# A decoder layer on one core: attention's long scans in two parts, two weight blocks prepared earlier, and other banks for the first down product

## The chip, the cores and the metric

The kernel runs on one core of a Trainium2 chip. Its engines each have their own instruction queue: TensorE (PE, with PEld for its weight loads), VectorE (DVE), ScalarE (ACT), GpSimd (POOL) and SyncE (SP, which here issues nearly all DMAs). The metric is the device time of one execution in microseconds.

## The reference

One layer on 1024 tokens of width 1024, all in float32: an SSD (Mamba-2) head group and a stick-breaking attention head group in parallel, their outputs joined and projected, then an MLP, then a last norm. What the change touches:

```python
logits = jnp.einsum("bthd,bshd->bhts", qb, kb) * scale      # a block of 128 queries, all keys up to them
log_beta = jax.nn.log_sigmoid(logits)
log_1m_beta = jnp.where(mask, jax.nn.log_sigmoid(-logits), 0.0)
suffix = lax.cumsum(log_1m_beta, axis=-1, reverse=True) - log_1m_beta
att = jnp.where(mask, jnp.exp(log_beta + suffix), 0.0)      # then att @ v
...
x = x + jnp.concatenate([y_ssd, y_att], axis=-1) @ w_out
h = rmsnorm(x, norm_mlp_g)
x = x + jnp.square(jax.nn.relu(h @ w_up)) @ w_down
return rmsnorm(x, final_norm_g)
```

## The kernel before

**Products.** Every large product is made of three matmuls on float32r halves (high x high, high x low, low x high). An operand is split by a copy to float32r (the high half) and a subtraction (the low half): `split(raw, hi, lo, where)`, L105, with the copy on ACT and the subtraction on DVE ("vec") or POOL ("poollo"), or both on POOL ("pool").

**Order.** The program is written for a scheduling framework that puts each engine's instructions into one fixed queue ahead of time, by program order, by priorities (`tc.high_priority` pulls an instruction forward) and by when it reckons them ready; waits between engines are semaphores. On the chip each queue runs in order. So an instruction that is cut into two can also change the places of its neighbours in the queue.

**Stages.** Projection, convolution and SSD come first. Then attention, in eight pairs of heads (`hp`): for each pair the queries are worked on in groups `g` of two 128-query blocks, while PE interleaves the projection of the next pair's q, k and v (`qkv`, matmuls L161 to L163). In attention, the logits go to PSUM (L528 to L531), ACT makes `m` = sigmoid(-logit) (L548) and `a` = sigmoid(logit) (L549), DVE runs a reversed running product over `m` in place (the scan, L539), and multiplies `a` by it (L541). PE then transposes `a` (L599) into a bank of the tag `tr` (two banks), ACT copies out the high half `ath` (L602), DVE makes the low half `atl` (L603), and PE multiplies with v (L615, L616) into a bank `ps_b` (two banks), which DVE's `yt` (L629) empties. L602, L603 and L629 are of high priority. For `g` = 1 a tile holds two heads of 384 or of 512 columns; for `g` = 2 and 3 a tile holds one head of 640, 768, 896 or 1024 columns, and the logits of its columns from 512 on go through PSUM and ACT first. `short` has scans of 128 and 256 columns. So a pair has two scans each of the eight lengths.

**Mix.** The joined output is projected in eight blocks (`mix_block`, L734 to L736); L783 adds each result to the residual `x1`. In the last block (7) the first half of the rows is normed as it is finished (`norm_a`, `norm_b`) and transposed into `B11` and `B21` (`block`, L858 to L862).

**MLP.** Up and down products are Strassen-like products P1 to P7 of 512-wide blocks. The up product runs over `steps`; the first 12 (`pre`) are the P1 and P2 of the first six blocks, while the remaining operands (T1 to T4, B22) are still being made by `block_sums`, `norm_b` and `block` in `second_half`. `wblock` makes the weight operand of a step: a load of a whole row block `wf` (1024 columns, two buffers), and a split of 512 of them. The results are squared by ACT (L950, L951) and, with sums by DVE (`u_sums`, L970), written to memory (`ub`). The pools `prb` (before) and `pe` (after) share memory, as do the PSUM banks of the tags `tr`, `x`, `y` and the six banks `a` of the down product. `mm` has two banks of its own for the whole kernel; in the up product P1 and P2 use them.

**Down product.** Seven products P1, P2, P5, P6, P7, P3, P4, each with four banks and 16 operands `n` (two blocks each: `raw` from `ub`, and a block of w_down). Operands 0 to 3 are made before the up product ends. `prepare(n)` issues loads nine ahead and makes operands six ahead. `load_t(kp)` loads a block that product P5 needs; for operands 4 to 15 of P1 it is also P1's own.

Of the kernel before, what the change touches and what calls it, by code (L numbers as in the profile page):

```python
# [8 lines left out]
F32 = mybir.dt.float32  # L9
F32R = mybir.dt.float32r  # L10
BF16 = mybir.dt.bfloat16
AF = mybir.ActivationFunctionType
ALU = mybir.AluOpType
# [3 lines left out]
P = 128  # L17
# [7 lines left out]
NW = 4  # L25
# [25 lines left out]
def trunk(ctx: ExitStack, tc, x, wct, wdt, cols, g_mix, g_mlp, g_fin, wout, wup, wdown, out):  # L51
    nc = tc.nc
    mm, act, vec, pool = nc.tensor.matmul, nc.scalar, nc.vector, nc.gpsimd
# [14 lines left out]
    ws = ctx.enter_context(tc.tile_pool(name="ws", bufs=2))  # L68

    def bank(tag):  # L70
        if tag == "mm":
            return psm.tile([P, 512], F32, name="ps_mm", tag="mm")
        n, w = banks[tag]
        return banks["pool"].tile([P, 512 * w], F32, name=f"ps_{tag}", tag=tag, bufs=n)
# [30 lines left out]
    def split(raw, hi, lo, where):  # L105
        if where == "pool":
            pool.tensor_scalar(out=hi, in0=raw, scalar1=1.0, scalar2=0.0, op0=ALU.mult, op1=ALU.add)  # L107
            pool.tensor_tensor(out=lo, in0=raw, in1=hi.bitcast(F32), op=ALU.subtract)  # L108
        else:
            act.copy(out=hi, in_=raw)  # L110
            e = vec if where == "vec" else pool
            e.tensor_tensor(out=lo, in0=raw, in1=hi.bitcast(F32), op=ALU.subtract)  # L112
# [13 lines left out]
    def rms_scale(ss, r):  # L126

        pool.tensor_scalar(out=r, in0=ss, scalar1=1.0 / 1024.0, scalar2=EPS, op0=ALU.mult, op1=ALU.add)
        pool.tensor_tensor(out=r, in0=r, in1=mhalf[:, : r.shape[-1]], op=ALU.pow)
# [383 lines left out]
    class Group:  # L513
# [19 lines left out]
        def weigh(self, a, m, segments):  # L533

            end = sum(segments)
            cut = end
            for k in segments[::-1]:
                mv = m[:, cut - k:cut][:, ::-1]
                vec.tensor_tensor_scan(mv, mv, mv, 1.0, ALU.mult, ALU.min)  # L539
                cut -= k  # L540
            vec.tensor_tensor(out=a[:, 0:end - 1], in0=a[:, 0:end - 1], in1=m[:, 1:end], op=ALU.mult)  # L541

# [140 lines left out]
    for k in range(len(slots) + LATE):  # L683
        if k < len(slots):
            n, r, b = slots[k]
# [92 lines left out]
    def mix_block(b, operands, lag=0):  # L778


        def store(ps, tt, n):
            o, c = x1[tt][:, n], (0 if b < 4 else 8) + tt
            vec.scalar_tensor_tensor(out=o, in0=ps, scalar=rr[:, c:c + 1], in1=o, op0=ALU.mult, op1=ALU.add)  # L783

        return accumulate(*operands, store, lag)
# [43 lines left out]
    def norm_a(tt):  # L829

        sq = pr.tile([P, D], F32, name="sq", tag="sq")
        ss = pr.tile([P, 1], F32, name="ss", tag="ss", bufs=4)
        r = pr.tile([P, 1], F32, name="r", tag="r", bufs=4)
        nc.sync.dma_start(out=x1d[tt], in_=x1[tt])
        act.activation(out=sq, in_=x1[tt], func=AF.Square, accum_out=ss)
        rms_scale(ss, r)
        scale[tt] = r

    def norm_b(tt):

        vec.scalar_tensor_tensor(out=x1[tt], in0=x1[tt], scalar=scale[tt][:, 0:1], in1=gm, op0=ALU.mult, op1=ALU.mult)
# [13 lines left out]
    def block(nm, src, j, tag):  # L855
        ps = bank(tag)
        for k in range(4):
            nc.tensor.transpose(out=ps[:, k * P:(k + 1) * P], in_=src[:, k * P:(k + 1) * P], identity=ident)  # L858
        pv = ps.rearrange("p (k t) -> p k t", k=4)
        dh, dl = [h[:, :, j * P:(j + 1) * P] for h in hb[nm]]  # L860
        act.copy(out=dh, in_=pv)
        vec.tensor_tensor(out=dl, in0=pv, in1=dh.bitcast(F32), op=ALU.subtract)  # L862

    scale = {}
    pc_.close()
    pr = pr_.enter_context(tc.tile_pool(name="pr", bufs=1, side="right", reuse_waits="tile"))
    gm = pr.tile([P, D], F32, name="gm", tag="gm")
# [2 lines left out]
    for i, _ in enumerate(mix_block(7, nxt)):  # L870
        for tt in range(4):
            if i == 2 * tt + 3:
                norm_a(tt)
            if i == 2 * tt + 4:
                norm_b(tt)
            if i == 2 * tt + 6:
                block("B11", x1[tt][:, k0], tt, "tr")
                block("B21", x1[tt][:, k1], tt, "tr")
        if i in (11, 13):
            norm_a(i // 2 - 1)  # L880
    norm_b(4)
    block("B11", x1[3][:, k0], 3, "tr")
    block("B21", x1[3][:, k1], 3, "tr")
# [7 lines left out]
    def second_half():  # L891

        turn = ("tr", "x", "y") * 7
        for tt in range(4, 8):
            made = block_sums(tt)
            if tt < 7:
                norm_b(tt + 1)
            for n, (nm, src) in enumerate(made):
                block(nm, src, tt - 4, turn[5 * (tt - 4) + n])
                if (5 * (tt - 4) + n) % 2:  # L900
                    yield
# [6 lines left out]
    for m in range(0, 16, 2):  # L908
# [1 line left out]
        if m < EARLY:  # L910
            head = [(m, "P6"), (m + 1, "P6")]
        steps += head + [(m + e, p) for p in ("P7", "P5", "P4", "P3") for e in range(2)]
    wraw, wsum, wop, acc, kept = {}, {}, {}, {}, {}
    loaded = set()

    def wload(i, name, early):
# [111 lines left out]
    def b_of(kp, nm):  # L1028
        return wdown[2 * kp + int(nm[1]) - 1][:, (int(nm[2]) - 1) * 512:int(nm[2]) * 512]
# [6 lines left out]
    def load_t(kp):  # L1036
        t_of[kp] = pe.tile([P, 512], F32, name="t", tag="t", bufs=16)
        nc.sync.dma_start(out=t_of[kp], in_=b_of(kp, "B11"))

    def d_load(n, pl, bufs):  # L1040

        p, kp = slots[n]
        a = load_raw(ub[UB[A_OF[p]] + kp], pl, bufs)
        b = None
        if p == "P1":
            if n < 4:
                b = load_raw(b_of(kp, "B11"), pl, bufs)
            else:
                load_t(kp)
        elif p == "P6":  # L1050
            b22_of[kp] = pe.tile([P, 512], F32, name="b22", tag="b22", bufs=16)
            nc.sync.dma_start(out=b22_of[kp], in_=b_of(kp, "B22"))
        elif p != "P3":
            b = load_raw(b_of(kp, {"P2": "B21", "P5": "B12", "P7": "B12", "P4": "B21"}[p]), pl, bufs)
        braw[n] = a, b
# [26 lines left out]
        split(b, o[2], o[3], "vec")  # L1082
        bops[n] = o

    loaded_ops = set()
    blocks = second_half()
    pu, pu_ = None, ExitStack()
    for s in range(len(pre)):
# [29 lines left out]
    gf = pr.tile([P, D], F32, name="gf", tag="gm")  # L1118
    psum_phase(a=(6, 1))

    def final_norm(tt):
        sq = pr.tile([P, D], F32, name="sq", tag="sq")
        ss = pd.tile([P, 1], F32, name="ss", tag="ss", bufs=4)
        r = pd.tile([P, 1], F32, name="r", tag="r", bufs=4)
        act.activation(out=sq, in_=x2[tt], func=AF.Square, accum_out=ss)
        rms_scale(ss, r)
        vec.scalar_tensor_tensor(out=x2[tt], in0=x2[tt], scalar=r[:, 0:1], in1=gf, op0=ALU.mult, op1=ALU.mult)
        nc.sync.dma_start(out=out[tt * P:(tt + 1) * P, :], in_=x2[tt])
# [32 lines left out]
    later2 = []  # L1161
    NRAW, LOAD, MAKE, TAIL = 8, 9, 6, 4
    loads = made = len(bops)
    for kp in range(4):
        load_t(kp)
    nc.sync.dma_start(out=gf, in_=g_fin)

    def prepare(n):
        nonlocal loads, made
        while loads < min(n + LOAD + 1, len(slots)):  # L1170
            d_load(loads, pe, NRAW)
            loads += 1
        while made < min(n + MAKE + 1, len(slots)):
            d_make(made)
            made += 1

    def d_mm(ps, tt, o, first, last):
        t = slice(tt * P, (tt + 1) * P)
        mm(out=ps, lhsT=o[0][:, t], rhs=o[2], start=first, stop=False)  # L1179
        mm(out=ps, lhsT=o[0][:, t], rhs=o[3], start=False, stop=False)  # L1180
        mm(out=ps, lhsT=o[1][:, t], rhs=o[2], start=False, stop=last)  # L1181

    for j, p in enumerate(ORDER):
        pss = [bank("mm" if j % 2 and tt > 1 else "a") for tt in range(4)]
        end = 16 - (TAIL if p == "P4" else 0)
        for kp in range(end):
            n = 16 * j + kp
            prepare(n)
            if kp > 0 and later2:
                later2.pop(0)()  # L1190
            o = bops.pop(n)
            for tt in range(4):
                d_mm(pss[tt], tt, o, kp == 0, kp == 15)
        for tt in range(4):
            for kp in range(end, 16):
                d_mm(pss[tt], tt, bops[16 * j + kp], False, kp == 15)
            done(p, tt, pss[tt])
            if p == "P4" and tt > 0:
                final_norm(3 + tt)
            if p == "P4" and tt == 3:  # L1200
                sq = pr.tile([P, D], F32, name="sq", tag="sq")
                for n, ac in ((n2, last_sums[1]), (n1, last_sums[0])):
                    act.activation(out=sq[:, n], in_=x2[7][:, n], func=AF.Square, accum_out=ac)
# [71 lines left out]
```

## Time and profile before

| | us |
|---|---|
| three runs, median (lowest to highest) | 1777.83 (1775.32 to 1777.92) |
| the profiled execution, its own time | 1772.97 |
| its span, first to last instruction | 1771.3 |
| PE busy in the span | 1710.7 |
| DVE busy | 1276.8 |
| ACT busy | 813.8 |
| POOL busy | 518.5 |

The mean granted TensorE clock is 0.993 of full speed. PE is busy for 97% of the span, so some 60 us are left in which it does nothing; nearly 27 us of them lie in the first 40 us and the last 20 us (PE busy 26.66 of 40.00 and 9.46 of 20.00), which the change doesn't touch. A time is read best against PE's waits, stage by stage.

### The profile page before, as it was taken

Reading aid. Unit: us, or ns where it says so; the run is one execution under the profiler, and the core shown is the slowest. Engines: PE = TensorE matmul, PEld = TensorE weight load, DVE = VectorE, ACT = ScalarE, POOL = GpSimd, SP = SyncE. Lnnn points to the kernel's source line nnn. Section 1 sums busy time; section 2 is a strip of 40 time slices with the busy share of each in tenths; the row PEclk is TensorE's granted clock in tenths of the full one; section 3 lists DMA queues with packets and bytes.
Section 4 is the critical chain, followed back from the end, with each engine's and each line's share of the span. In section 5 each row is a group of like instructions: output and inputs, shape, how many; then the busy total and the mean of one; then the engine's idle time right before and its main releaser. Section 6 shows DMA issues by size and latency. Waiting matters only on the chain.

```text
span 1771.3 us, 23843 instructions
## 1 busy us (share of the span) xinstructions
PE 1710.7 (97%) x8492; PEld 1396.8 (79%) x8492; DVE 1276.8 (72%) x1771; ACT 813.8 (46%) x1560; POOL 518.5 (29%) x601
## 2 busy tenths in 40 slices
PE   6999999998999999999999999999999999999997
PEld 5778878877778778778778888788888877888886
DVE  6587887459888888888775666967665656687775
ACT  5233133336667666666563121554455446444443
POOL 6222222053443443443464332410222200010221
PEclk9999999999999999999999999999999999999999
DMA  4101102130101100110135221455434449855454
GB/s 157 37 27 57 54 31 96 36 119 25 34 31 34 33 31 33 34 36 28 60 122 210 103 89 71 159 167 208 156 143 143 159 155 320 281 167 153 162 167 148
DMA packets 90839, 189.39 MB, mean 107 GB/s; under 512 B 10080, under 2 KB 14432, under 8 KB 90720
## 3 DMA queue, kind: packets, MB, share of 16 engines
q1 hardware_dynamic: 90576, 187.61, 31.1%
q8 instruction: 67, 1.10, 0.3%
q14 instruction: 52, 0.43, 0.1%
q10 hardware_dynamic: 144, 0.26, 0.0%
HBM read 137.50 MB, written 50.33 MB: 106 GB/s over the span
## 4 chain that ended last, share of the span: by engine, by line
PE 81%; DVE 10%; POOL 2%; ACT 2%; DMA 2%; issue 2%; SPq 0%; DVEq 0%; POOLq 0%; ACTq 0%
PE ps_mm L161 8%; PE ps_mm L163 8%; PE ps_mm L162 8%; PE ps_a L1179 4%; PE ps_a L1181 4%; PE ps_a L1180 4%; DVE m L539 4%; PE ps_a L734 3%; PE ps_a L736 3%; PE ps_a L735 3%; PE ps_tr L599 3%; PE ps_x L987 3%; PE ps_x L985 3%; PE ps_x L986 3%; DVE a L541 2%; PE ps_mm L987 2%
## 5 line engine op out<-in xcount | busy, mean ns | idle before, releaser
L161 PE MATMUL ps_mm<-hhi,whi 128*128 128x512 f32 (+1 forms) x784 | 321.4, 410 | 0.0
L163 PE MATMUL ps_mm<-hhi,wlo 128*128 128x512 f32 (+1 forms) x784 | 308.4, 393 | 0.0
L162 PE MATMUL ps_mm<-hlo,whi 128*128 128x512 f32 (+1 forms) x784 | 307.5, 392 | 0.0
L539 DVE TENSOR_TENSOR_SCAN m<-m 128x512 f32<-128x512 f32 (+7 forms) x128 | 182.5, 1450 | 29.0 <-ACT m L548 28.4
L163 PEld LDWEIGHTS ps_mm<-hhi,wlo 128*128 128x128 f32 x784 | 148.2, 189 | 32.1 <-issue 2.4
L161 PEld LDWEIGHTS ps_mm<-hhi,whi 128*128 128x128 f32 x784 | 148.8, 190 | 19.8 <-issue 2.9
L162 PEld LDWEIGHTS ps_mm<-hlo,whi 128*128 128x128 f32 x784 | 149.0, 190 | 18.3 <-issue 1.5
L108 POOL TENSOR_TENSOR wlo<-raw,whi 128x512 fp32r<-128x512 f32 x90 | 138.3, 1537 | 7.4
L112 POOL TENSOR_TENSOR wlo<-wf,whi 128x512 fp32r<-128x512 f32 x48 | 65.4, 1364 | 243.2 <-ACT whi L110 243.2
L783 DVE SCALAR_TENSOR_TENSOR x<-ps_a,rr,x 128x512 f32<-128x512 f32 x128 | 93.7, 748 | 56.0 <-PE ps_a L736 46.8
L107 POOL TENSOR_SCALAR whi<-raw 128x512 fp32r<-128x512 f32 x90 | 67.9, 755 | 223.9 <-PE ps_mm L162 211.5
L603 DVE TENSOR_TENSOR atl<-ps_tr,ath 128x512 fp32r<-128x512 f32 (+1 forms) x160 | 100.6, 631 | 41.3 <-ACT ath L602 39.9
L110 ACT CAST op<-raw 128x512 fp32r<-128x512 f32 x131 | 78.0, 620 | 107.8 <-issue 48.4
L112 DVE TENSOR_TENSOR op<-raw,op 128x512 fp32r<-128x512 f32 x131 | 91.0, 716 | 37.3 <-ACT op L110 36.9
L1179 PE MATMUL ps_a<-op 128*128 128x512 f32 x278 | 109.0, 392 | 1.9 <-ACT uP L951 1.9
L1180 PE MATMUL ps_a<-op 128*128 128x512 f32 x278 | 108.8, 391 | 0.0
L1181 PE MATMUL ps_a<-op 128*128 128x512 f32 x278 | 108.7, 391 | 0.0
L548 ACT ACTIVATE m<-ps_a 128x384 f32<-128x384 f32 (+1 forms) x192 | 95.7, 498 | 25.0 <-PE ps_a L531 21.8
L599 PE MATMUL ps_tr<-ident,a 128*128 128x128 f32 x576 | 91.7, 275 | 14.3 <-DVE a L541 8.2
L602 ACT CAST ath<-ps_tr 128x512 fp32r<-128x512 f32 (+1 forms) x160 | 86.9, 545 | 35.9 <-PE ps_tr L599 34.0
L599 PEld LDWEIGHTS ps_tr<-ident,a 128*128 128x128 f32 x576 | 70.7, 140 | 37.5 <-DVE atl L603 9.5
L1136 POOL TENSOR_TENSOR x<-x,raw 128x512 f32<-128x512 f32 x16 | 26.4, 1657 | 248.5 <-DVE x L1144 113.9
(365 smaller groups left out, 4280.3 us busy)
## 6 DMA issues: line engine op xcount, KB each, us to landing
raw<-ub SPq DMA_DIRECT2D x112, 256.0 KB, 3.3
raw<-in_wct_dram SPq DMA_DIRECT2D x96, 256.0 KB, 2.6
wf<-in_wup_dram SPq DMA_DIRECT2D x38, 512.0 KB, 3.5
raw<-in_wdown_dram SPq DMA_DIRECT2D x68, 256.0 KB, 3.3
ub<-v SPq DMA_DIRECT2D x48, 256.0 KB, 2.0
raw<-in_wout_dram SPq DMA_DIRECT2D x32, 256.0 KB, 2.7
yl<-ygt SPq DMA_DIRECT2D x16, 512.0 KB, 4.4
ub<-uP SPq DMA_DIRECT2D x32, 256.0 KB, 2.0
```

The costliest lines, as they stand in the source:

```text
L108: pool.tensor_tensor(out=lo, in0=raw, in1=hi.bitcast(F32), op=ALU.subtract)
L112: e.tensor_tensor(out=lo, in0=raw, in1=hi.bitcast(F32), op=ALU.subtract)
L161: mm(out=o, lhsT=whi[:, wc], rhs=hhi[:, k, n], start=(k == 0), stop=False)
L162: mm(out=o, lhsT=whi[:, wc], rhs=hlo[:, k, n], start=False, stop=False)
L163: mm(out=o, lhsT=wlo[:, wc], rhs=hhi[:, k, n], start=False, stop=(k == KT - 1))
L539: vec.tensor_tensor_scan(mv, mv, mv, 1.0, ALU.mult, ALU.min)
L548: act.activation(out=m[:, o:o + w], in_=src, func=AF.Sigmoid, scale=-1.0)
L599: nc.tensor.transpose(out=tp[:, o:o + P], in_=a[:, c:c + P], identity=ident)
L603: vec.tensor_tensor(out=tl[:, o:], in0=tp[:, o:], in1=th[:, o:].bitcast(F32), op=ALU.subtract)
L1179: mm(out=ps, lhsT=o[0][:, t], rhs=o[2], start=first, stop=False)
L1180: mm(out=ps, lhsT=o[0][:, t], rhs=o[3], start=False, stop=False)
L1181: mm(out=ps, lhsT=o[1][:, t], rhs=o[2], start=False, stop=last)
```

## The change

Three edits. (1) In `weigh`, a scan of more than 384 columns becomes two: one over the last `h` columns from 1.0, then one over the others, which starts from the first one's last column, `m[:, cut - h]`. The lengths become 512 = 256 + 256, 640 = 256 + 384, 768 = 384 + 384, 896 = 384 + 512 and 1024 = 512 + 512 (the part that runs first is named first). (2) In the last mix block, after its turns 6 and 8, the weight operands of up steps 0 and 1 (P1 of blocks 0 and 1) are loaded into `raw` buffers and split, instead of at the start of the up product, from `wf`. The loads of `wf` stay for P2. (3) The first down product, and every second one after it, takes two `mm` banks and two `a` banks, and those between take four `a` banks; the loads `load_t(0)` to `load_t(3)` and of `gf` are moved from ahead of the product into its first turns, behind `prepare`.

```diff
@@ weigh
             for k in segments[::-1]:
-                mv = m[:, cut - k:cut][:, ::-1]
-                vec.tensor_tensor_scan(mv, mv, mv, 1.0, ALU.mult, ALU.min)
+                h = k // 256 * 128 if k > 384 else k
+                for p, start in ((cut - h, 1.0), (cut - k, m[:, cut - h:cut - h + 1]))[:1 + (h < k)]:
+                    mv = m[:, p:cut if p == cut - h else cut - h][:, ::-1]
+                    vec.tensor_tensor_scan(mv, mv, mv, start, ALU.mult, ALU.min)
                 cut -= k
@@ the last mix block
-    scale = {}
+    scale, wop = {}, {}
...
         if i in (11, 13):
             norm_a(i // 2 - 1)
+        if i in (6, 8):
+            raw = ws.tile([P, 512], F32, name="raw", tag="raw", bufs=2)
+            nc.sync.dma_start(out=raw, in_=wup[i - 6][:, 0:512])
+            hi = ws.tile([P, 512], F32R, name="whi", tag="whi", bufs=NW)
+            lo = ws.tile([P, 512], F32R, name="wlo", tag="wlo", bufs=NW)
+            split(raw, hi, lo, "poollo")
+            wop[i // 2 - 3] = hi, lo
...
-    wraw, wsum, wop, acc, kept = {}, {}, {}, {}, {}
+    wraw, wsum, acc, kept = {}, {}, {}, {}
...
-    loaded_ops = set()
+    loaded_ops = set(wop)
@@ the down product
-    for kp in range(4):
-        load_t(kp)
-    nc.sync.dma_start(out=gf, in_=g_fin)
...
     for j, p in enumerate(ORDER):
-        pss = [bank("mm" if j % 2 and tt > 1 else "a") for tt in range(4)]
+        pss = [bank("mm" if j % 2 == 0 and tt < 2 else "a") for tt in range(4)]
         end = 16 - (TAIL if p == "P4" else 0)
         for kp in range(end):
             n = 16 * j + kp
             prepare(n)
+            if n < 4:
+                load_t(n)
+            if n == 4:
+                nc.sync.dma_start(out=gf, in_=g_fin)
```

## Rows read from the trace of the kernel before

**Rows 1.** PE's waits, whole span: releaser, us in total, times, longest us

```profile
PE ps_tr L599 <- DVE a L541: 8.2, 10, 1.0
PE ps_tr L599 <- DVE atl L603: 6.1, 8, 1.7
PE ps_b L615 <- DVE yt L629: 5.9, 3, 2.8
...
PE ps_a L1179 <- ACT uP L951: 1.9, 1, 1.9
PE ps_x L858 <- DVE x L849: 1.7, 1, 1.7
...
PE ps_mm L987 <- POOL wlo L112: 1.6, 1, 1.6
PE ps_a L1179 <- ACT whi L110: 1.6, 1, 1.6
```

**Rows 2.** Windows, attention: stretch; us; PE, PEld, DVE, ACT, POOL busy; clock; DMA; GB/s

```profile
525.00:590.00 65.00, 62.95 (x368) 51.63 (x367) 54.82 (x67) 41.77 (x94) 27.17 (x39) 1.00 0.11 33
```

**Rows 3.** DVE's groups by shape: count, busy us, mean ns, idle before

```profile
L783 DVE SCALAR_TENSOR_TENSOR x<-ps_a,rr,x 128x512 f32<-128x512 f32 x128 | 93.7, 748 | 56.0 <-PE ps_a L736 46.8 <-POOL rr L129 8.5
...
L603 DVE TENSOR_TENSOR atl<-ps_tr,ath 128x512 fp32r<-128x512 f32 x96 | 65.5, 684 | 35.6 <-ACT ath L602 35.1
...
L539 DVE TENSOR_TENSOR_SCAN m<-m 128x1024 f32<-128x1024 f32 x16 | 37.6, 2351 | 0.0
...
L539 DVE TENSOR_TENSOR_SCAN m<-m 128x512 f32<-128x512 f32 x16 | 18.7, 1208 | 0.4 <-ACT m L548 0.4
...
L539 DVE TENSOR_TENSOR_SCAN m<-m 128x256 f32<-128x256 f32 x16 | 10.7, 668 | 0.0
```

**Rows 4.** Timeline of DVE in that pair: start us, us, instruction

```profile
571.27 2.81 DVE L539 TENSOR_TENSOR_SCAN m<-m 128x896 f32<-128x896 f32 x1 [0.92 <-ACT m L548]
574.19 1.09 DVE L541 TENSOR_TENSOR a<-a,m 128x895 f32<-128x895 f32 x1
...
575.79 2.28 DVE L539 TENSOR_TENSOR_SCAN m<-m 128x1024 f32<-128x1024 f32 x1
...
579.76 1.20 DVE L541 TENSOR_TENSOR a<-a,m 128x1023 f32<-128x1023 f32 x1
```

**Rows 5.** Timeline of POOL in the same stretch

```profile
570.92 1.28 POOL L108 TENSOR_TENSOR wlo<-raw,whi 128x512 fp32r<-128x512 f32 x1
...
575.84 3.33 POOL L108 TENSOR_TENSOR wlo<-raw,whi 128x512 fp32r<-128x512 f32 x1
```

**Rows 6.** Timeline of PE at the start of the up product

```profile
1126.58 0.66 PE L858 MATMUL ps_x<-ident,x 128*128 128x128 f32 x4 [1.73 <-DVE x L849]
...
1129.49 0.79 PE L987 MATMUL ps_mm<-B11h,wlo 128*128 128x512 f32 x1 [1.59 <-POOL wlo L112]
...
1132.64 0.42 PE L985 MATMUL ps_mm<-B11h,whi 128*128 128x512 f32 x1
```

**Rows 7.** Timeline of DVE there

```profile
1124.63 0.69 DVE L862 TENSOR_TENSOR B11l<-ps_tr,B11h 128x512 fp32r<-128x512 f32 x1 [0.30 <-ACT B11h L861]
```

**Rows 8.** Busy time of the engines (columns as in rows 2) in two stretches of 2 us

```profile
1130.00:1132.00 2.00, 2.00 (x6) 1.53 (x5) 2.00 (x4) 0.94 (x2) 1.50 (x2) 0.50 0.00 0
1454.00:1456.00 2.00, 2.00 (x6) 1.58 (x5) 1.54 (x3) 0.00 (x0) 0.00 (x0) 0.50 0.99 364
```

**Rows 9.** SP's queue at the start of the down product

```profile
1458.66 1.84 SPq L1038 DMA_DIRECT2D t<-in_wdown_dram  x4
...
1461.02 0.43 SPq L1038 DMA_DIRECT2D t<-in_wdown_dram  x1
```

**Rows 10.** PE there

```profile
1467.17 1.20 PE L1179 MATMUL ps_a<-whi 128*128 128x512 f32 x4 [1.58 <-ACT whi L110]
```

**Rows 11.** DMA issues of the whole kernel: count, KB each, median us to landing

```profile
raw<-ub SPq DMA_DIRECT2D x112, 256.0 KB, 3.3
```

**Rows 12.** The same between 1440 and 1480 us

```profile
t<-in_wdown_dram SPq DMA_DIRECT2D x16, 256.0 KB, 5.4
```

## The prediction

> **What bounds the kernel now.** I read the page first: PE is busy for 1710.7 of 1771.3 us, so no other engine sets the end, and a change is worth only what it takes from PE's idle time, or from the stretches in which PE's clock is low. Then PE's waits [rows 1], because each names the engine that came late; then the stretches around the three edits, for which of these waits lie there.
>
> In attention the waits are on DVE: for `a` (8.2 us in ten waits), for `atl` (6.1 in eight) and for `yt` (5.9 in three). The reader is to see in the window of one head pair [rows 2] how little that is: PE does nothing for 2.05 of 65 us. DVE is busy for 54.82, and from one long scan to the next product it has hardly a gap [rows 4]. So DVE isn't the bound there, but it is close to it, and what lengthens its queue in such a stretch reaches PE soon.
>
> At the start of the up product PE waits 1.7 us for DVE and 1.6 for POOL's `wlo`, at the start of the down product 1.9 for ACT's `uP` and 1.6 for ACT's `whi` [rows 1]. After the first two and after the 1.9 the granted clock falls to half (0.50, six matmuls in 2 us) [rows 8], so these stops cost more than the waits. After the second 1.6 I saw no such fall.
>
> **Edit 2, the first up operands: 3.5 us less.** In the queue of before, PE transposes T1 behind the wait for DVE, starts step 0 and stops again at its third matmul for `wlo` [rows 6]. With the operand there, the stop of 1.6 is gone. Step 0 also needs `B11l`, which ends at 1124.63 + 0.69 = 1125.32 [rows 7], while PE has been free since 1126.58 - 1.73 = 1124.85 [rows 6]. If the queue lets step 0 go ahead of T1, 0.5 of the 1.7 is left, a gain of 1.2. The half clock lasts from 1129.49 to 1132.64 [rows 6], 3.15 us, of which half, 1.6, is lost. Together 1.2 + 1.6 + 1.6 = 4.4. Against it: DVE is busy without a gap there (2.00 of 2.00) [rows 8], so PE, earlier by these microseconds, finds the next transposed blocks less ready; I take 0.9 off. What is added is two loads of 256 KB on SP (behind stores of `x1d` in program order, seven to nine turns of the mix block before its end), two casts on ACT, and two subtractions on POOL of the form that takes 1.28 [rows 5]. ACT and POOL have room in that stage. If POOL's two hold up DVE there, the last rows' norm comes up to 2.6 later, and that would eat most of the gain. Bounds: 0.5 to 4.4.
>
> **Edit 3, the first down product: 3.5 us less.** PE's first stop is for a bank whose last reader is ACT's square of the last up block (the 1.9). Before, one turn of three matmuls runs first. With two banks from `mm` and the one that was free before, three turns do, six matmuls more. The eight matmuls of the dip [rows 6] start 3.15 / 7 = 0.45 apart, so 0.225 at the full clock: six are 1.3. So 1.3 of the 1.9 goes, and the dip of the clock with it, which I cost like the other at 1.6: 2.9. Then the load of operand 4. Its `t` is issued at 1461.02, behind `gf` and four other `t` [rows 9], and PE gets it at 1467.17 [rows 10], 6.15 later. Without those ahead it could be issued where they were, at 1458.66, a gain of 2.36: PE gets it at 1464.8. With 1.5 MB less in flight (`gf` has 512 KB) the landing, 5.4 here [rows 12], should also come nearer to the 3.3 which such a load takes over the whole kernel [rows 11], by at most 2.1: 1462.7. PE, 2.9 earlier, asks for it at 1467.17 - 1.58 - 2.9 = 1462.7 too. So the end of this stop moves by 2.4 to 4.5, and it alone counts, since both stops lie in a row: I take 3.5. The moved loads are not wanted before P5 and the last norm; they cost nothing while loads run ahead of PE. Bounds: 0.5 (the loads wait for the memory of `prb` just as long, and the longer stop brings a dip) to 5.
>
> **Edit 1, the scans: 2 us less, and little certainty.** A pair has two scans each of 512, 640, 768, 896 and 1024 columns, so 80 are cut in all. Durations of the parts come from their own length [rows 3]: 2 x 668 - 1208 = 128 ns more for 512, 2 x 1208 - 2351 = 65 ns more for 1024. The second part must wait for the first: a product that depends on its scan starts 574.19 - (571.27 + 2.81) = 0.11 us after it [rows 4]. No row has a scan that starts from a column. The nearest is an operation with a column operand, 748 against 684 ns [rows 3], though it isn't the same operation; so 0 to 0.06. That makes 0.17 to 0.3 per cut, and I take 0.25: 20 us more of DVE's time in all, 2.5 in a pair, whose 54.82 then become some 57 of 65. I exclude a gain from faster scanning, as the parts' sum is above the whole.
>
> The errata section of the Trainium skill's page "VectorE: DVE Perf Modes" speaks against the cut: a fixed cost per instruction, about 150 cycles, is paid by each part. At 0.96 GHz that is an estimated 0.156 us, more than the 65 to 128 ns of the rows; 80 times it is 12.5 us, and the sum below would be about 1 us worse.
>
> What the cut gives is places in DVE's queue: `atl` and `yt` are of high priority and can now go between the parts instead of behind 2.28 us of scan [rows 4]. If that removes half of their 12.0 us of waits [rows 1], the gain is 6. What it costs is the product at the end: `a`, for which PE waits, ends at 579.76 + 1.20, and two cut scans are ahead of it in one gapless queue [rows 4]. That is 2 x 0.25 = 0.5 a pair, 4 in all. The early start of the part of 896 whose columns ACT makes first saves nothing, as POOL holds that scan up until 1.28 of its own are over [rows 4, 5]. Net 2 less; ends: 17 less (nearly all waits of DVE's three gone) to 12 more (the slow rival).
>
> **Sum.** 3.5 + 3.5 + 2 = 9 from the profiled execution's 1772.97 gives 1764. That execution is 4.9 below the median of the runs, 1777.83, so for the median 1769 (likeliest 1764 to 1774).
>
> **The rivals.** *DVE pays all back:* the cuts lengthen the gapless stretch, in which there are four (two of 512 follow), and all of it reaches PE: 8 x 4 x 0.25 = 8 us. Then -7 + 8 = +1: 1779, no change. For it is DVE's load [rows 2]; against it that PE idles only 2 us a pair today. Chance 0.19.
>
> *POOL comes in between (slower):* POOL's subtraction that began at 575.84 took 3.33 instead of 1.28 [rows 5], ending about 1.1 after the scan of 1024 [rows 4]: it stood still while the scan ran. And the scan of 896, begun while POOL was at work, took 2.81 [rows 4], more than 2.28 for 1024. The two exclude each other, instruction by instruction. A cut scan lets POOL in halfway, and the second part waits out 1.28. With the one scan of 1024 and the one of 896 ahead of `a` hit, that is 2 x 1.28 + 0.5 = 3.1 a pair at worst; less about 0.7 that DVE can fill with `atl`, 2.4: 8 x 2.4 = 19, so -7 + 19 = +12: 1790. It decides from 1.4 us a pair on (11 in all). Against it: the part for which POOL waits is the same work, and it only goes earlier, which shortens other stops. Chance 0.14. The Trainium skill's "SBUF — State Buffer", section "Who interferes with whom", states it as a rule: a VectorE instruction with two SBUF inputs and a GpSimd one that reads SBUF hold a shared port by turns, each for a whole instruction. The trace agrees with 3.33 against 1.28.
>
> *The gaps do all:* `atl`, `yt` and `a` come in time everywhere, 17 less beside 7: 1754. For it: the two of high priority no longer stand behind a whole scan; against it, `a` is not of high priority and its queue grows. Chance 0.12.
>
> *The early edits do nothing* (step 0 still goes behind T1 and the clock dips; the down loads wait for memory): 1 less instead of 7, with the scans' 2: 1775, within what can be told. Chance 0.05.
>
> **How the numbers follow.** The forecast has the rest, 0.50. A measurement of this kernel can tell some 0.2%, 3.6 us, from no change. Faster: 0.50 + 0.12 = 0.62, and 0.02 for the better half of the others' spread, 0.64; same 0.22; slower 0.14. The range leaves out most of the slow rival and half of the best: 1756 to 1784. It is this wide because of the scans alone.
>
> **What would show it.** In the changed profile: 80 more scans, pieces of 256 at 0.67, 384 near 0.9 and 512 at 1.2 us, with `atl` or `yt` between pieces. PE's waits on `atl` and `yt` down from 12 to about 6, on `a` up from 8 to about 12. The waits for `wlo` L112 and `uP` gone, no clock of 0.50 at either start, and operand 4 on PE some 3.5 us earlier, counted from the end of the up product. Pieces of scan that last 1.3 longer than their kind, next to POOL's subtractions, would be the slow rival. What makes the prediction wrong above all: another order of DVE's queue, since one new wait in a pair comes eight times.

## The result and the profile after

The changed kernel takes 1794.22 us (median of four runs, 1793.63 to 1794.29) against 1777.2 of the kernel before (1775.32 to 1777.92): the ratio is 1.0100, with a 95% interval of 1.0087 to 1.0112. It is slower by 17 us, where 9 less was forecast, and it lies above the range. Of all runs in this document one was disturbed, 8033.73 us of a kernel that otherwise takes some 1760; it is left out. The profiled execution took 1793.63 (span 1791.9); that of before lies some 4 us below its other runs, so the two traces differ by 20.6.

Where they came from is read from landmarks, the same PE instruction found in both traces. The end of attention moved from 941.94 to 964.96, so by 23.0; the start of the last mix block by 24.3; the end of the up product by 21.8; operand 4 of the down product by 19.15. So attention lost 23, the mix up to its last block another 1.3, and the starts of the up and down products gave back 2.5 and 2.65. Behind operand 4 another 1.45 is lost, up to the 20.6 at the end. The end of attention, before and after:

```profile
941.94 1.84 PE L717 MATMUL ps_tr<-ones,zacc 128*128 128x2 f32 x16
...
964.96 1.84 PE L719 MATMUL ps_tr<-ones,zacc 128*128 128x2 f32 x16
```

PE's waits in the changed kernel, columns as in [rows 1]:

```profile
PE ps_tr L601 <- DVE a L543: 12.7, 10, 1.7
PE ps_tr L601 <- DVE atl L605: 10.7, 18, 1.6
...
PE ps_b L617 <- DVE yt L631: 5.0, 3, 2.3
PE ps_a L528 <- ACT a L551: 4.2, 7, 0.8
...
PE ps_mm L1184 <- ACT whi L110: 2.6, 1, 2.6
```

The wait for `a` rose from 8.2 to 12.7, which is what the prediction had costed (12). The wait for `atl` should have fallen and rose from 6.1 to 10.7, in 18 places where there were eight, and the wait for ACT's `a`, 0.7 before, is 4.2. The waits for `wlo` L112 and `uP` are gone.

Windows of the changed kernel, columns as in [rows 2]: one pair of heads, three stretches of 4 us behind a wait for `a`, then the start of the up and of the down product:

```profile
529.00:596.00 67.00, 63.78 (x368) 51.93 (x368) 58.49 (x78) 41.52 (x94) 27.21 (x40) 1.00 0.10 32
...
654.00:658.00 4.00, 4.00 (x15) 2.94 (x14) 2.74 (x5) 2.33 (x5) 1.08 (x2) 0.57 0.00 1
722.00:726.00 4.00, 3.78 (x13) 2.90 (x14) 2.24 (x5) 1.39 (x4) 1.78 (x3) 0.57 0.07 27
790.00:794.00 4.00, 2.95 (x18) 2.38 (x19) 3.54 (x5) 2.67 (x7) 2.52 (x4) 1.00 0.26 63
...
1150.00:1152.00 2.00, 2.00 (x14) 1.72 (x13) 2.00 (x4) 1.32 (x4) 1.38 (x2) 1.00 1.03 299
...
1488.00:1490.00 2.00, 2.00 (x6) 1.51 (x6) 1.99 (x4) 1.84 (x4) 0.00 (x0) 0.50 1.06 403
```

The same 368 matmuls take 67 us instead of 65, and DVE is busy for 58.49 of them instead of 54.82 [rows 2]: 3.7 more a pair where 2.5 were expected. The clock in the second and third row is new there: 0.57 over 4 us, part of them at the half level (0.50, which is 1.2 GHz of 2.4). Multiplying in windows of 2 us what is missing from the full clock by their length, attention loses 10.2 us to the clock; before, it lost 1.7 (one fall, between 876 and 880). PE's idle time there went from 23.5 to 34.1. (Both are counted from 394 us to the end of attention.) These two, 8.5 and 10.6, are 19 of the 23; the other 4 I didn't resolve.

DVE's scans and products in all, before (two rows) and after (two rows), then its groups by shape in the changed kernel, columns as in [rows 3]:

```profile
L539 DVE TENSOR_TENSOR_SCAN m<-m 128x512 f32<-128x512 f32 (+7 forms) x128 | 182.5, 1450 | 29.0 <-ACT m L548 28.4
L541 DVE TENSOR_TENSOR a<-a,m 128x767 f32<-128x767 f32 (+3 forms) x88 | 95.2, 1082 | 4.9 <-ACT ath L602 0.5
...
L541 DVE TENSOR_TENSOR_SCAN m<-m 128x384 f32<-128x384 f32 (+3 forms) x208 | 201.9, 987 | 20.7 <-ACT m L550 16.4
L543 DVE TENSOR_TENSOR a<-a,m 128x767 f32<-128x767 f32 (+3 forms) x88 | 109.0, 1239 | 6.8
...
L541 DVE TENSOR_TENSOR_SCAN m<-m 128x384 f32<-128x384 f32 x80 | 82.6, 1042 | 11.1 <-ACT m L550 10.5
L541 DVE TENSOR_TENSOR_SCAN m<-m 128x512 f32<-128x512 f32 x48 | 68.0, 1416 | 3.2
L541 DVE TENSOR_TENSOR_SCAN m<-m 128x256 f32<-128x256 f32 x64 | 45.7, 726 | 6.1 <-ACT m L550 5.6
...
L543 DVE TENSOR_TENSOR a<-a,m 128x895 f32<-128x895 f32 x16 | 23.5, 1468 | 1.7
```

DVE and POOL in the stretch of the changed kernel that answers to [rows 4, 5]:

```profile
574.81 2.43 DVE L541 TENSOR_TENSOR_SCAN m<-m 128x384 f32<-128x384 f32 x2
575.00 1.17 POOL L107 TENSOR_SCALAR whi<-raw 128x512 fp32r<-128x512 f32 x1
576.25 2.07 POOL L108 TENSOR_TENSOR wlo<-raw,whi 128x512 fp32r<-128x512 f32 x1
577.34 1.93 DVE L543 TENSOR_TENSOR a<-a,m 128x895 f32<-128x895 f32 x1
...
579.80 3.37 DVE L541 TENSOR_TENSOR_SCAN m<-m 128x512 f32<-128x512 f32 x2
579.84 2.25 POOL L108 TENSOR_TENSOR wlo<-raw,whi 128x512 fp32r<-128x512 f32 x1
...
583.20 0.42 DVE L631 TENSOR_TENSOR yt<-ps_b,y 64x256 f32<-64x256 f32 x1
...
584.85 1.21 DVE L543 TENSOR_TENSOR a<-a,m 128x1023 f32<-128x1023 f32 x1
```

The scans take 19.4 us more, as costed (20); the products, which were not costed, take 13.8 more. A piece of 512 takes 1416 ns on the mean, not 1208. The timeline shows why: POOL's `wlo` begins 0.04 after the first half of the scan of 1024 and goes between the halves, so the two take 3.37 instead of 2.28 [rows 4]. The product of 895 columns, 1.09 before [rows 4], meets the other `wlo` and takes 1.93. And the two halves lie side by side (x2): neither `atl` nor `yt` stands between them; `yt` follows the second.

PE in the changed kernel: the wait for `a` in six pairs, then the starts of up and down, as in [rows 6, 10]:

```profile
518.97 0.52 PE L601 MATMUL ps_tr<-ident,a 128*128 128x128 f32 x3 [1.48 <-DVE a L543]
...
586.21 0.52 PE L601 MATMUL ps_tr<-ident,a 128*128 128x128 f32 x3 [1.48 <-DVE a L543]
...
653.44 0.52 PE L601 MATMUL ps_tr<-ident,a 128*128 128x128 f32 x3 [1.48 <-DVE a L543]
...
722.22 0.83 PE L601 MATMUL ps_tr<-ident,a 128*128 128x128 f32 x3 [1.48 <-DVE a L543]
...
791.05 0.52 PE L601 MATMUL ps_tr<-ident,a 128*128 128x128 f32 x3 [1.48 <-DVE a L543]
...
858.30 0.52 PE L601 MATMUL ps_tr<-ident,a 128*128 128x128 f32 x3 [1.48 <-DVE a L543]
...
1148.97 0.73 PE L994 MATMUL ps_mm<-B11h,whi 128*128 128x512 f32 x2 [0.24 <-ACT B11h L863]
...
1472.35 0.40 PE L996 MATMUL ps_y<-B22h,wlo 128*128 128x512 f32 x1
1472.59 0.40 PE L1184 MATMUL ps_mm<-op 128*128 128x512 f32 x1
...
1486.32 0.77 PE L1184 MATMUL ps_mm<-whi 128*128 128x512 f32 x2 [2.64 <-ACT whi L110]
```

Step 0 of the up product (1148.97) goes without a stop for `wlo` or the norm (0.24 for `B11h` is left), and the down product runs on from the up product without a stop, up to operand 4.

### The profile page after: what moved, and what is told of

The parts are those of the page before. It is cut to its first block, busy times and chain, and to the rows that moved or that the text cites. A ratio compares the mean times of both kernels' runs of the same rounds, so it can differ in the third digit from the quotient of the medians.

```text
span 1791.9 us, 23962 instructions
## 1 busy us (share of the span) xinstructions
PE 1721.9 (96%) x8492; PEld 1401.1 (78%) x8492; DVE 1306.6 (73%) x1851; ACT 812.8 (45%) x1560; POOL 507.4 (28%) x601
## 4 chain that ended last, share of the span: by engine, by line
PE 57%; DVE 12%; issue 4%; ACT 3%; DMA 1%; POOL 0%; DVEq 0%; POOLq 0%; ACTq 0%; SPq 0%
DVE m L541 5%; PE ps_a L1184 4%; PE ps_a L1186 4%; PE ps_a L1185 4%; PE ps_a L736 3%; PE ps_a L738 3%; PE ps_a L737 3%; PE ps_x L996 2%; PE ps_x L995 2%; PE ps_x L994 2%; PE ps_mm L162 2%; PE ps_mm L163 2%; PE ps_mm L161 2%; DVE a L543 2%; DVE atl L605 2%
## 5 line engine op out<-in xcount | busy, mean ns | idle before, releaser
L541 DVE TENSOR_TENSOR_SCAN m<-m 128x384 f32<-128x384 f32 (+3 forms) x208 | 201.9, 987 | 20.7 <-ACT m L550 16.4
L112 POOL TENSOR_TENSOR wlo<-wf,whi 128x512 fp32r<-128x512 f32 x46 | 61.9, 1347 | 244.2 <-ACT whi L110 244.2
L112 DVE TENSOR_TENSOR op<-raw,op 128x512 fp32r<-128x512 f32 x131 | 93.0, 732 | 34.7 <-ACT op L110 34.2
L601 PE MATMUL ps_tr<-ident,a 128*128 128x128 f32 x576 | 92.6, 276 | 23.5 <-DVE a L543 12.7
L543 DVE TENSOR_TENSOR a<-a,m 128x767 f32<-128x767 f32 (+3 forms) x88 | 109.0, 1239 | 6.8
L551 ACT ACTIVATE a<-ps_a 128x384 f32<-128x384 f32 (+1 forms) x192 | 97.1, 505 | 0.6
L1186 PE MATMUL ps_a<-op 128*128 128x512 f32 x250 | 97.3, 389 | 0.0
L1184 PE MATMUL ps_a<-op 128*128 128x512 f32 x250 | 97.3, 389 | 0.0
```

The source lines that it names most:

```text
L541: vec.tensor_tensor_scan(mv, mv, mv, start, ALU.mult, ALU.min)
L551: act.activation(out=a[:, o:o + w], in_=src, func=AF.Sigmoid)
L601: nc.tensor.transpose(out=tp[:, o:o + P], in_=a[:, c:c + P], identity=ident)
```

## The experiments

Each ratio is to the kernel before, run on the same chip. The theories: the scans alone lose the time, by what a cut costs DVE itself (the second part waits for the first), by GpSimd's instructions that come in between, or by both. Where a kernel computes something else, its expectation says what it leaves out.

**The parts of the change by themselves.** The first kernel has edit 1 alone, the second edits 2 and 3, then one with edit 2 and one with edit 3.

```diff
@@ second kernel, against the changed one
-                h = k // 256 * 128 if k > 384 else k
-                for p, start in ((cut - h, 1.0), (cut - k, m[:, cut - h:cut - h + 1]))[:1 + (h < k)]:
...
+                mv = m[:, cut - k:cut][:, ::-1]
+                vec.tensor_tensor_scan(mv, mv, mv, 1.0, ALU.mult, ALU.min)
```

> The cut scans alone, without the two other edits. In the trace of the changed kernel attention ends 23 us later than before, the mix 1.3 later, the starts of the up and down products give 2.5 and 1.1 back. If the loss belongs to the cut scans: about 24 us above the kernel before. If the early operands and moved loads had a part in it: less than 20.

> The two other edits without the cut: by the trace of the changed kernel 3 to 4 us below the kernel before (2.5 at the start of the up product, about 1 at the start of the down product). The prediction's terms would give 7 below.

> Only the two up operands made early. By the traces of the changed kernel and of the one without the cut, the up product ends 2.5 us earlier, counted from the last mix block: 2 to 4 below before. If the two edits gain their 10 us together from one stop that either removes: 8 or more.

> Only the first down product in other banks and the moved loads. By the traces operand 4 comes 2.7 to 3.8 earlier after the up product, with 1.6 lost again by the clock where the stop is long: 1 to 6 below before.

Measured: scans alone 1802.43 (ratio 1.0141, 1.0118 to 1.0165), so 25 more; edits 2 and 3 1767.58 (0.9943, 0.9931 to 0.9956), 10 less; edit 2 alone 1773.97 (0.9977, 0.9967 to 0.9987) and edit 3 alone 1773.26 (0.9977, 0.9967 to 0.9988), 4 less each. The two edits together gave more than either number forecast for them (3 to 4, and 7). With the scans' edit the other two still give 1802.4 - 1794.2 = 8. So the whole loss is edit 1's. In the trace of the first kernel attention ends 25.1 later than before, in that of the second 0.6 later.

**Fewer cuts.** Only 896 and 1024 are cut, 32 of the 80.

```diff
-                h = k // 256 * 128 if k > 384 else k
+                h = k // 256 * 128 if k > 768 else k
```

> Only the scans of 896 and 1024 columns are cut (32 of the 80 cuts). If each cut costs alike: 32/80 of the loss, 8 to 11 us above before. If GpSimd coming in between is the cost (its subtractions meet these two scans of a pair): most of it, 15 to 22. If only the order of the queues matters: no rule, and most likely a number off both.

Measured, without edits 2 and 3: 1786.51 (1.0052, 1.0036 to 1.0067), 9 more. 32/80 of 25 is 10: this one point fits a loss in proportion to the cuts, and it isn't these long scans alone that make it (15 to 22 was expected then).

**A cut whose second part waits for nothing.** It starts from 1.0.

```diff
-                for p, start in ((cut - h, 1.0), (cut - k, m[:, cut - h:cut - h + 1]))[:1 + (h < k)]:
+                for p, start in ((cut - h, 1.0), (cut - k, 1.0))[:1 + (h < k)]:
```

> The cut scans alone, but the second part starts from 1.0 and not from the first part's last column (so the product of the later keys is left out for the earlier ones): same number and lengths of instructions, no wait of the second part for the first. If the wait between the parts is the cost (0.11 us seen plus the overlap that is lost, some 0.2 of 0.25 us a cut): at most a third of the loss is left, 4 to 9 us above before. If the cost is the instructions themselves, or GpSimd coming in between: within 5 us of the cut scans alone.

Measured: 1787.13 (1.0050, 1.0036 to 1.0063). Of the 25 us, 15 go with the dependence and 9 stay without it. That is the upper end of the first forecast (4 to 9), and not the second (within 5 of 1802): the wait between the parts is the larger cost, but not the only one.

**GpSimd nearly off the port.** In attention ACT makes the weights' high halves, and GpSimd writes zeros instead of reading (its additions to `sacc_a` and in the gate stay). Three kernels: whole scans, all cuts, and all cuts from 1.0.

```diff
@@ split
+        elif where == "light":
+            act.copy(out=hi, in_=raw)
+            pool.memset(lo.bitcast(F32), 0.0)
@@ qkv, zgate
-            w = unit(wct[16 + 3 * hp + which], "pool" if hp else "vec")
+            w = unit(wct[16 + 3 * hp + which], "light" if hp else "vec")
...
-                                pool.tensor_scalar(out=t[b, n], in0=t[a, n].bitcast(F32), scalar1=1.0, scalar2=0.0,
-                                                   op0=ALU.mult, op1=ALU.add)
+                                pool.memset(t[b, n].bitcast(F32), 0.0)
...
-        w = unit(wct[40 + j], "pool")
+        w = unit(wct[40 + j], "light")
```

> The scans whole, and GpSimd off the shared port in attention: in attention's projections the weights' high half is copied by ScalarE, and their low half and the second copies of the keys are zeros that GpSimd only writes (so the small terms of these products are left out). Both theories: within 10 us of the kernel before; if VectorE's waits for GpSimd delay TensorE there, a little faster. It is the measure for the next run.

> The same with all 80 cuts (it leaves out the same terms). If GpSimd coming in between the parts is the cost: at most 10 us slower than the run with whole scans and light GpSimd. If it is the cut itself (fixed part of each instruction, and the second part's wait for the first): 18 to 25 us slower, as with GpSimd at work.

> The light kernel (GpSimd writes zeros in place of the weights' low halves and of the second key copies, and ACT makes the high halves) with all 80 scans cut, but the second part starts from 1.0, so that the product of the later keys is left out for the earlier ones. It is the fourth corner beside: whole scans at 1762.1, cut scans that start from the column 1773.5, and, with GpSimd at work, 1777.5, 1802.4, and 1787.1 for the cut that starts from 1.0. If GpSimd and the dependence are separate prices that add, the dependence costs 15 with GpSimd at work and so 15 here: 1759 or no slower than whole scans. If the dependence costs so much only because GpSimd's instruction slips in at the gap before the second part, this kernel gains little against the cut that starts from the column: 1770 to 1773, with 80 gaps of 0.1 less on DVE, most of them covered. Place in the queue (the parts are free to lie elsewhere) may add or take 2.

Measured: whole scans 1759.88, the median of three runs (0.9905, 0.9888 to 0.9922; the expectation above counts from 1762.1, a median with the run of 8033.73 in it); cut 1773.51 (0.9981, 0.9971 to 0.9991); cut from 1.0 1762.55 (0.9911, 0.9899 to 0.9922). Whole scans gained 17 us, more than the 10 that were expected at most. In us against whole scans under the same GpSimd, by the ratios, and in brackets by the end of attention in the traces:

| | GpSimd at work | GpSimd nearly off the port |
|---|---|---|
| second part waits for the first | +25 (25.1) | +13.5 (11.2) |
| second part waits for nothing | +9 (9.4) | +1 (0.0) |

The ends of attention are these: GpSimd at work, cut and cut from 1.0, then GpSimd nearly off, whole, cut and cut from 1.0 (for whole scans with GpSimd at work it is the 941.94 above):

```profile
967.04 1.84 PE L719 MATMUL ps_tr<-ones,zacc 128*128 128x2 f32 x16
...
951.37 1.84 PE L719 MATMUL ps_tr<-ones,zacc 128*128 128x2 f32 x16
...
926.94 1.84 PE L719 MATMUL ps_tr<-ones,zacc 128*128 128x2 f32 x16
...
938.14 1.84 PE L721 MATMUL ps_tr<-ones,zacc 128*128 128x2 f32 x16
...
926.90 1.84 PE L721 MATMUL ps_tr<-ones,zacc 128*128 128x2 f32 x16
```

The numbers of the table have margins of 2 to 4 us by the intervals. With GpSimd nearly off, a cut that waits for nothing costs PE nothing that can be told. The wait for the first part costs 11 to 13.5, GpSimd's reads cost 9 where the second part waits for nothing, and together they cost 25: their sum, or up to 5 more, which the runs can't tell from none. In the traces the excess is the clock's: by windows of 2 us attention loses 10.3 us to it with both causes, 3.4 with either one, and 1.7 with whole scans, so both together lose some 5 more than the sum.

So neither forecast for the cut with GpSimd nearly off came (at most 10, or 18 to 25): both causes are at work. Of the last two theories the second falls (a cut from 1.0 that gains little, 1770 to 1773). The first holds in direction, as that cut is no slower than whole scans; its price of 15 for the dependence measured 11 to 12. DVE's scans in all, with GpSimd nearly off, whole, cut and cut from 1.0:

```profile
L541 DVE TENSOR_TENSOR_SCAN m<-m 128x512 f32<-128x512 f32 (+7 forms) x128 | 170.3, 1357 | 21.8 <-ACT m L550 20.6
...
L543 DVE TENSOR_TENSOR_SCAN m<-m 128x384 f32<-128x384 f32 (+3 forms) x208 | 191.6, 938 | 11.3 <-ACT m L552 6.5
...
L543 DVE TENSOR_TENSOR_SCAN m<-m 128x384 f32<-128x384 f32 (+3 forms) x208 | 181.4, 908 | 10.0 <-ACT m L552 8.2
```

So 80 cuts add 21.3 us to DVE's scans, 0.27 each, and 11.1, 0.14 each, where the second part waits for nothing. The timeline shows one length beside it. A scan of 1024 columns, whole:

```profile
558.71 2.28 DVE L541 TENSOR_TENSOR_SCAN m<-m 128x1024 f32<-128x1024 f32 x1
```

The same in the kernel with all cuts (x2 are the two halves):

```profile
561.24 2.61 DVE L543 TENSOR_TENSOR_SCAN m<-m 128x512 f32<-128x512 f32 x2
```

And in the kernel whose second halves start from 1.0:

```profile
558.81 2.33 DVE L543 TENSOR_TENSOR_SCAN m<-m 128x512 f32<-128x512 f32 x2
```

2.28, 2.61, 2.33: for these halves the dependent start costs 0.28 and the second instruction 0.05. With GpSimd at work the two halves take 3.37 where it comes in between, 1.09 more than whole. In the kernel before, one of the 16 whole scans of 1024 was hit (3.38; the others take 2.28 to 2.32, and the mean of all is the 2351 ns of [rows 3]).

**Versions that might beat both.** Edits 2 and 3 with whole scans, and GpSimd keeps only the subtractions of these weights: ACT makes the high halves (in the gate of the SSD stage too). In the second kernel ACT also makes the second key copies.

```diff
-            w = unit(wct[16 + 3 * hp + which], "pool" if hp else "vec")
+            w = unit(wct[16 + 3 * hp + which], "poollo" if hp else "vec")
...
-        w = unit(wct[40 + j], "pool")
+        w = unit(wct[40 + j], "poollo")
@@ in the second kernel
-                                pool.tensor_scalar(out=t[b, n], in0=t[a, n].bitcast(F32), scalar1=1.0, scalar2=0.0,
-                                                   op0=ALU.mult, op1=ALU.add)
+                                act.copy(out=t[b, n], in_=t[a, n].bitcast(F32))
```

> Nothing left out. Whole scans with edits 2 and 3 (1767.6), and the high halves of the later weights of projection, gate and attention are made by ACT instead of GpSimd, which keeps the subtractions. If DVE's stops beside GpSimd are what makes PE wait in attention, some half of the 15 us that GpSimd's full removal gave is had: 1759 to 1764, with PE's waits for a and atl down by a third. If ACT, busy for 42 of 65 us in a pair, becomes late with m, ath or the weights' halves, the waits go over to ACT and the time is 1768 to 1775.

> Nothing left out. As the one before, and the second copies of the keys are made by ACT too. If GpSimd's share of the port is the cause, another 2 to 4 us less than the one before, 1756 to 1762. If ACT is late, more than the one before, above 1766.

Measured: 1759.33 (0.9894, 0.9881 to 0.9907), 19 less than the kernel before, the fastest here that computes everything and inside its forecast; and 1781.51 (1.0019, 1.0011 to 1.0028) for the second, which loses it all again. PE's waits in the first:

```profile
PE ps_tr L599 <- DVE atl L603: 6.7, 11, 1.6
PE ps_b L615 <- DVE yt L629: 5.8, 9, 1.8
...
PE ps_tr L599 <- DVE a L541: 2.8, 4, 0.9
```

PE's waits in the second:

```profile
PE ps_tr L598 <- DVE atl L602: 11.0, 10, 1.6
...
PE ps_tr L598 <- DVE a L540: 5.4, 4, 3.6
PE ps_b L614 <- DVE yt L628: 4.9, 8, 1.8
PE ps_a L527 <- ACT a L548: 3.2, 6, 0.5
```

In the first, `a` comes in time more often (8.2 to 2.8), and no fall of the clock is left in attention. In the second, ACT is late. DVE's own waits, for `ath`, show it. In the first kernel:

```profile
DVE atl L603 <- ACT ath L602: 43.5, 32, 3.1
```

And in the second:

```profile
DVE atl L602 <- ACT ath L601: 63.2, 40, 3.8
```

## Why the prediction was wrong

**The step that failed is edit 1's term, "net 2 less"**, in both halves: a gain of 6 that did not come, and a cost of 4 that was 25. The terms of edits 2 and 3 held.

*The gain of 6 did not come.* It rested on `atl` and `yt` going between the parts. In the steady pair `atl` never does, and `yt` between four of the ten; the other halves lie side by side. They do so too where the second half starts from 1.0 and waits for nothing, so it isn't the dependence that keeps them together; why the order comes out so is not shown. The step took a possible place in the queue for a taken one. PE's wait for `atl` rose by 4.6 instead of falling, that for `yt` fell by 0.9. Of PE's waits on `atl` and `yt` together 12.0 became 15.7, not 6.

*The price of a cut was about right, what of it reaches PE was not.* I took 0.25 from a range of 0.17 to 0.3; with GpSimd nearly off the port it measured 0.27 on the mean of all cuts, and 0.33 for the halves of 1024. (The lower end rested on the mean of 2351 ns, which has the hit scan in it.) But of 20 us more on DVE I let 4 reach PE, two cuts in each pair; of the 21.3 measured, 11.2 to 13.5 did. That is nearer to the rival "DVE pays all back", which has four cuts a pair and 8. Of the Trainium skill's fixed cost per instruction (page "VectorE: DVE Perf Modes", errata section), 0.156 us by the estimate there, this case shows: 0.14 on the mean for cuts that wait for nothing, 0.05 for two halves of 512 side by side, which together take less than twice one of them (2.33 against 2 x 1.208 [rows 3]), and 0.27 for cuts that wait.

*GpSimd came in between.* This is the slow rival, to which I gave 0.14. Its picture was right: 3.37 for the two halves at 579.80, POOL's 2.25 beside them. It was priced at 19 for attention, 1790 in all; the scans alone measured 25, of which 11 to 14 is what GpSimd at work adds (25 - 13.5 by the runs, 25.1 - 11.2 by the traces). So 1790 came near 1794 in part by luck: this mechanism has 11 to 14 of its 19, and the dependence the rest of the 25. Against it I had argued that POOL's work is the same and only goes earlier. But the product of 895 columns, whole before (1.09), now meets POOL's next instruction and takes 1.93: the earlier start moves the collision, it does not remove it. The Trainium skill's page "SBUF — State Buffer", section "Who interferes with whom", has it as a rule, that VectorE work with two SBUF inputs and GpSimd's reads exclude each other; the rows of the two engines above agree (3.37 for the halves beside a `wlo` of 2.25, 1.93 for the product beside one of 2.07).

*The clock was not costed at all for attention.* With PE's longer waits the half clock came at six places, where there had been one: 8.5 us, which are part of the prices above. I had priced this at the two starts and not where the same kind of wait returns in each pair.

**Edit 2 held.** 3.5 was predicted; counted from the last mix block the up product ends 2.5 earlier in the changed kernel, 3.25 in the kernel with edit 2 alone, and 4 by its runs. Step 0 goes ahead of T1, as hoped, and no window at the start is at 0.50 (1150 to 1152: 1.00). New is a wait of 0.55 for the norm of the last rows, at 1154.38.

**Edit 3 held.** 3.5 was predicted, from 2.4 to 4.5 for operand 4; it came 2.65 earlier, counted from the end of the up product, and 3.1 with edit 3 alone. One step in it was off: `gf` is still issued ahead of the first `t` (1478.80 before 1481.06), and the other `t` are behind. And I saw no fall of the clock at the second stop; now there is one (0.50 at 1488 to 1490), which loses 1.7 by windows of 2 us, as much as the one behind the first stop did before; so in this trace some 1 us of the 2.65 is left. With edit 3 alone the fall comes too, with edits 2 and 3 it doesn't, and operand 4 is 3.8 earlier.

**The range.** It ended at 1784, below the 1790 of a rival whose two ingredients [rows 4, 5] had been seen in the trace. What stays open: 4 of the 23 us that attention lost, which are neither idle time of PE nor the clock, and why the same wait brings the half clock in some pairs and not in others.

The idle time of the first 40 and last 20 us, named with the profile before, is 13.34 + 10.54 = 23.9 us and not nearly 27; no term of the forecast used it.

## What to carry to other kernels

Cutting a long instruction gives a place in the queue only if another instruction is known to take it; here most halves stayed side by side, and where the second needs the first, each cut costs a dependent start, 0.28 us for halves of 512. Where two engines exclude each other, as DVE and GpSimd do here (3.37 instead of 2.28), an instruction boundary is also an opening for the other engine: count whose instruction is waiting there, and what it will meet next, before cutting. And look first at who holds the engine up: moving the copies of the weights' high halves from GpSimd to ACT gave 8 us (1767.58 to 1759.33), where cutting DVE's own work cost 25.

## What the runs showed of the hardware

The same wait does not always bring the half clock. In six of the rows of PE above the wait for `a` is 1.48, each in another pair; after 653.44, 722.22 and 858.30 the granted clock fell (0.57 in the windows at 654 and 722), after 518.97, 586.21 and 791.05 it stayed at 1.00. So it fell in three of six pairs; with edit 1 alone, where PE has the same wait of 1.48 in six pairs, in five. Before, PE waited 2.81 at 424.26 with the clock at 1.00 in the 6 us behind it. A pair without such a fall is 67.24 long, one with it 68.8, so a fall costs about 1.6.

A GpSimd instruction that only writes did not hold up DVE here: where it writes zeros, all 16 whole scans of 1024 took 2.28 or 2.29, the one above (558.71) beside memsets from 559.71 on. With most of GpSimd's reads in attention gone, and whole scans, the kernel takes 17 us less than before (0.9905), about as much as the whole change cost, though ACT got more to do. The runs don't separate in this what the reads cost DVE from what the weights cost that come in another way: PE's wait for `whi` from POOL, 2.6 us before, is gone with them.
